# Values and keys of the scans turned by blocks of 32x32 and DMAs instead of on TensorE; the low-rank columns in four groups of output rows

## The chip, the cores and the metric

The kernel runs on one core of a Trainium2 chip. The metric is the device time of one execution in microseconds (us). The kernel before was run three times; the median is what counts. One further execution was taken by the hardware profiler, and all rows of the trace are from that one. Lines written L876 are lines of the kernel before.

## What is computed

The reference is one inference step of a decoder layer: a SwiGLU feed-forward block, a mixer, and a second feed-forward block, each with an RMSNorm before and after. There are 256 prompt tokens and 8 samples of 4 tokens, together 288 columns, and a model width of 2048. The mixer has 4 GLA heads (128 keys, 256 values, decays from 16 low-rank columns) and 8 HGRN heads (128 keys, 128 values). Both are recurrences per head:

```python
# S_t = diag(exp(log_a_t)) S_{t-1} + k_t^T v_t ; o_t = q_t S_t
q, k, v, a_lr, r, hq, hf, hi, hg = jnp.split(proj, _split_points(), axis=-1)
log_alpha = jax.nn.log_sigmoid((a_lr @ gla_w_up + gla_b).astype(jnp.float32)) / GLA_TAU
...
s_new = (jnp.exp(last[:, :, 0, :])[..., None] * s
         + jnp.einsum('bhsd,bhsv->bhdv', ki * jnp.exp(last - cum), vi))
```

The outputs are the tokens and the final states of every head, for the prompt (which starts from zero) and for each sample.

## The kernel before

Activations lie with features on the 128 partitions and the 288 token columns along the free dimension: 16 tiles `x[k]` and 16 tiles `y[k]`. Every large product is done in split fp32: a weight unit of 128x1024 is loaded (`raw`, 512 KB, on SyncE's queue), ScalarE rounds it to `wh` (L96) and VectorE takes the rest `wl` (L97); three matmuls (L548 to L550) then give hi x hi, hi x lo and lo x hi. Three raw units and four split ones are held ahead (`RAW_BUFS`, `HL_BUFS`). `block` (L539) runs four 128-row output tiles over all k tiles of the contraction, and calls `tick(k)` after each k tile. For the last unit of a block the four outputs are finished first, and its ticks follow together.

The mixer's work around the recurrences is done in these ticks. `tick` (L1295) first pops one entry of `turns`, then takes one step of the oldest unfinished generator `scan`, then one entry from each list in `later` that was there at the tick's start. So small matmuls, evacuations and DMAs of a scan are strung between the main matmuls of the next blocks. There are six scans: two of GLA (two heads each) and four of HGRN (two heads each). The order of the projection blocks is qk0, v0, qk1, v1, hfq0, hi0, hfq1, hi1, hfq2, hfq3 and then four gate blocks. A scheduler sets the order of the instructions on each engine from this order of issue and its own estimate of when an operand is ready; each engine then runs its queue in that order, and waits on semaphores.

What the change touches:

- `ev_v` (L892) evacuates a value block of 4 tiles (v0, v1, hi0, hi1). VectorE scales each tile into `y` (L897) and the sample columns, three times over, into `v3` (L898). The entry `turn` then transposes the tile on TensorE with `by_token` (L873): two transposes of 128 prompt tokens (L876) and one of the 96 tripled sample columns (L877). ScalarE copies the result to `Vt` (tokens on partitions) and `V32`, and `stack` (L879) splits the sample part into `Vs`.
- `key_t` and `key_e` (L1139, L1144) do the same for the keys of each of a scan's two heads: three transposes, ScalarE's copy into `kd` (L1148), and `stack` into `ks`.
- `final(a)` (L1181) multiplies `kd` with `Vt` to the prompt's final state, and stores it from GpSimd's queue. It is called in the scan's own steps: for the first head when the second one's keys are turned, for the second head in the scan's last steps. The sample states are stored from GpSimd's queue too (L1206).
- `a_lr` (L1332) forms the low-rank columns in v0's tick 13: 32 matmuls of the split inputs `xh[k]`, `xl[k]` (L1336) with a stationary tile that holds the rounded and the remaining part of the 16 columns. VectorE scales them (L1337), and the split result `alr` feeds `gla_decay` (L1346), whose matmul (L1350) starts the decays.

DMAs are issued by SyncE (weights, states), GpSimd (stores, small loads) and ScalarE (two small loads). The last feed-forward block already turns its input and output by VectorE's transposes of 32x32 blocks (L660, L662) and DMAs that put the blocks in their places (L671, L675).

Of the kernel before, what the change touches and what calls it, by code (L numbers as in the profile page):

```python
# [16 lines left out]
P = 128  # L17
TP = 256
TS = 32
# [106 lines left out]
def trunk_kernel(ctx, tc, x_prompt, x_sample, state_gla, state_hgrn, norm_gains, f1_in, f1_out, f2_in, f2_out,  # L126
# [115 lines left out]
    x = [xpool.tile([P, T], F32, name=f"x{k}") for k in range(KT)]  # L242
    y = [xpool.tile([P, T], F32, name=f"y{k}") for k in range(KT)]
    xh = [xpool.tile([P, T], F32R, name=f"xh{k}") for k in range(KT)]
# [346 lines left out]
    def xrhs(k):  # L591
        return xh[k], xl[k]
# [183 lines left out]
    def mixer(pn, border):  # L776
        with ExitStack() as mx:
# [25 lines left out]

            aw32, alr32 = y[KT - 2:], y[KT - 3]

            ahl = gp.tile([P, 1024], F32R, name="ahl", tag="V")
# [10 lines left out]

            def split_lr():

                av = ahl[:, 0:32 * KT].rearrange("p (k c) -> p k c", c=32)  # L820
                with tc.issue_after(pn.split[0]), tc.issue_after(pn.split[1]):
                    S.activation(av[:, :, 0:16], araw, AF.Copy)
                    V.tensor_tensor(av[:, :, 16:32], araw, av[:, :, 0:16].bitcast(F32), op=ALU.subtract)

# [47 lines left out]

            def by_token(tp, src, src3):  # L873

                for t in range(2):
                    PE.transpose(tp[:, t * P:(t + 1) * P], src[:, t * P:(t + 1) * P], ident)  # L876
                PE.transpose(tp[0:96, TP:TP + P], src3, ident)  # L877

# [6 lines left out]
            def vtiles(nm):  # L885
                vs32.append(vs32.pop(0))
                return (gp.tile([P, 2, 512], F32, name=f"V{nm}", tag="V"), vs32[-1],
                        gp.tile([96, 512], F32R, name=f"Vs{nm}", tag="Vs"))

            turns = []  # L890

            def ev_v(Vt, V32, Vs, y0=8):  # L892
                def ev(f, ps):

                    vt = y[y0 + f]
                    v3 = tmp.tile([P, 3, TS], F32, name="v3", tag="v3", bufs=4)
                    V.tensor_tensor(vt[:, 0:TP], ps[:, 0:TP], rt[:, 0:TP], op=ALU.mult)  # L897
                    V.tensor_tensor(v3, ps[:, TP:T].unsqueeze(1).broadcast_to([P, 3, TS]),  # L898
                                    rt[:, TP:T].unsqueeze(1).broadcast_to([P, 3, TS]), op=ALU.mult)

                    def turn():
                        tp = auxtile("tp_v")
                        by_token(tp, vt, v3.rearrange("p n t -> p (n t)"))
                        c = slice(f * P, (f + 1) * P)
                        S.activation(Vt[:, 0:2, c], tp[:, 0:TP].rearrange("p (t c) -> p t c", c=P), AF.Copy)
                        S.activation(V32[0:TS, c], tp[0:TS, TP:TP + P], AF.Copy)
                        stack(Vs[:, c], tp, TS)

                    turns.append(turn)
                return ev  # L910
# [9 lines left out]
            def scan(d, Vt, V32, Vs, gla, ytile0, s0, sp_out, ss_out):  # L920
# [216 lines left out]
                kds, bds, sqs, pos, mss = {}, {}, {}, {}, {}  # L1137

                def key_t(a):  # L1139
                    tp = auxtile("tp_k")  # L1140
                    by_token(tp, k[:, a, :], K3[:, a].rearrange("p n t -> p (n t)"))
                    return tp

                def key_e(a, tp):  # L1144

                    kd = sp[0].tile([P, 2, P], F32, name="kd", tag="kd")
                    ks = sp[0].tile([96, P], F32R, name="ks", tag="ks")
                    S.activation(kd, tp[:, 0:TP].rearrange("p (t c) -> p t c", c=P), AF.Copy)  # L1148
                    stack(ks, tp, 2 * TS)
                    kds[a] = kd, ks  # L1150

                def apart(a, b0):

                    src = kds[a][1] if gla else Vs[:, a * P:(a + 1) * P]
                    bd = sp[0].tile([96, nb, P], F32R, name="bd", tag="bd")
                    V.tensor_tensor(bd, src.bitcast(F32).unsqueeze(1).broadcast_to([96, nb, P]),
                                    bmask[:, b0:b0 + nb].unsqueeze(2).broadcast_to([96, nb, P]), op=ALU.mult)
                    bds[a, b0] = bd

                def out(a):  # L1160
                    vc = Vt[:, :, a * dv:(a + 1) * dv]

                    po, ss = auxtile("o"), auxtile("os")
                    for j in range(nv):
                        vj = vc[:, :, j * P:(j + 1) * P]
                        c0, c1, c2 = j * TP, j * TP + P, (j + 1) * TP
                        PE.matmul(po[:, c0:c1], vj[:, 0, :], Dg[:, 0, a, :], start=j == 0, stop=True, skip_group_check=True)
                        PE.matmul(po[:, c1:c2], vj[:, 0, :], X[:, a, :], start=False, stop=False, skip_group_check=True)
                        PE.matmul(po[:, c1:c2], vj[:, 1, :], Dg[:, 1, a, :], start=False, stop=True, skip_group_check=True)

                    for b in range(NB):
                        r = slice(b % 4 * TS, (b % 4 + 1) * TS)
                        PE.matmul(ss[r, 0:dv], qm[a][:, b * TS:(b + 1) * TS], states[a, b // nb * nb][:, b % nb, :],
                                  start=b < 4, stop=False, skip_group_check=True)
                    for i in range(4):
                        c = slice(i * dv // 4, (i + 1) * dv // 4)
                        PE.matmul(ss[i * TS:(i + 1) * TS, c], Ds[:, a, :], V32[:, a * dv + c.start:a * dv + c.stop],
                                  start=False, stop=True, skip_group_check=True)
                    pos[a] = po, ss

                def final(a):  # L1181

                    kd, vc = kds[a][0], Vt[:, :, a * dv:(a + 1) * dv]
                    ps = auxtile("st")
                    for t in range(2):
                        PE.matmul(ps[:, 0:dv], kd[:, t, :], vc[:, t, :], start=t == 0, stop=t == 1)
                    st = tmp.tile([P, dv], F32, name="st", tag="st", bufs=1)
                    S.activation(st, ps[:, 0:dv], AF.Copy)
                    G.dma_start(sp_out[a], st)

                def sample(a, b0):

                    s = states.pop((a, b0))
                    ks, bd = kds[a][1], bds.pop((a, b0))
                    ps = auxtile("sn")
# [66 lines left out]
                for a in range(2):  # L1262
                    tp = key_t(a)
                    load_state()
                    if a == 1:
                        final(0)
                        if gla:
                            new_state()
                    yield
# [15 lines left out]
                    new_state()  # L1285
                    if a == 1:
                        final(1)
                    yield
# [43 lines left out]
            def a_lr():  # L1332
                ps = mmtile("a_lr")
                for k in range(KT):
                    for i, m in enumerate(xrhs(k)):
                        PE.matmul(ps[:, 0:T], ahl[:, 32 * k:32 * k + P], m, start=k + i == 0, stop=k + i == KT)  # L1336
                V.tensor_tensor(alr32[0:32, :], ps[0:32, 0:T], rt[0:32, :], op=ALU.mult)  # L1337
                S.activation(alr[0:32, :], alr32[0:32, :], AF.Copy)
# [36 lines left out]
            for g in range(2):  # L1375
# [5 lines left out]
                if g == 0:  # L1381
                    vt = vtiles("g0")
                    block("v0", KT, xrhs, ev_v(*vt), 
                          tick=lambda k: (pn.tick1(k), split_lr() if k == 8 else a_lr() if k == 13 else None))
                    lower_bounds()
                    gla_decay(d, g)
                else:
                    gla_decay(d, g)
                    vt = vtiles("g1")
                    block("v1", KT, xrhs, ev_v(*vt), tick=tick)  # L1390
                gens.append((g, scan(d, *vt, True, 4 * g, state_gla[0][:, 2 * g:2 * g + 2],
                                     sgp[0, 0, 2 * g:2 * g + 2], sgs[0][:, 2 * g:2 * g + 2]), True))
            ds, vts = {}, {}
            for kind, g in HORDER:
                if kind == "hi":
                    written(g)
                    vts[g] = vtiles(f"h{g}")
                    block(f"hi{g}", KT, xrhs, ev_v(*vts[g], 8 + 4 * g), tick=tick)
                else:
                    written(g)  # L1400
                    ds[g] = group_tiles(f"h{g}")
                    block(f"hfq{g}", KT, xrhs, ev_hgrn(ds[g], g), tick=tick)
                for j in list(ds):
                    if j // 2 in vts:
                        c = slice((j % 2) * 256, (j % 2 + 1) * 256)
                        vt, v32, vs = vts[j // 2]
                        gens.append((2 + j, scan(ds.pop(j), vt[:, :, c], v32[:, c], vs[:, c], False, 8 + 2 * j,
                                                 state_hgrn[0][:, 2 * j:2 * j + 2], shp[0, 0, 2 * j:2 * j + 2],
# [113 lines left out]
```

## Time and profile before

| | |
|---|---|
| median of 3 runs | 2257.85 us (2257.52 to 2260.43) |
| the profiled execution | 2256.56 us |
| its span, first to last instruction | 2254.8 us |
| TensorE matmul busy | 2242.7 us, 17868 instructions |
| VectorE busy | 1379.7 us |
| ScalarE busy | 1021.4 us |
| GpSimd busy | 136.1 us |
| granted TensorE clock, mean | 0.998 |

The page's first part gives busy time by engine, its second the span in 40 slices, its fourth the chain of work that ended last. In rows in order of time the columns are: start, duration, engine, line, operation, what it writes and reads, shapes, count, and in brackets the idle time of its engine before it with what ended it. A matmul's duration is from its start to its modelled end; matmuls overlap, so the time that one costs TensorE is the distance to the next one's start. In rows by line the columns are busy us, mean ns of one, and idle time before.

### The profile page before, as it was taken

What the parts mean: (1) busy time and instruction counts of PE and PEld (TensorE: products, weight loads), DVE (VectorE), ACT (ScalarE), POOL (GpSimd) and SP (SyncE); (2) the same over time, 40 slices, a digit from 0 to 9 for tenths busy, and PEclk for the clock granted to TensorE, in tenths of its full rate; (3) what the DMA queues carried; (4) which work ended last, traced back from release to release, by engine and by line L of the source; (5) the groups of instructions that cost most, each with busy time, mean ns of one, the idle gap of its engine ahead of it and who ended that gap; (6) DMA issues with size and microseconds to landing.
All of it is one profiled execution on the core that took longest, in us unless ns stands there. A gap on an engine that the chain in (4) does not pass through costs nothing.

```text
span 2254.8 us, 43365 instructions
## 1 busy us (share of the span) xinstructions
PE 2242.7 (99%) x17868; PEld 2227.0 (99%) x17868; DVE 1379.7 (61%) x2251; ACT 1021.4 (45%) x1575; POOL 136.1 (6%) x250
## 2 busy tenths in 40 slices
PE   9999999999999999999999999999999999999998
PEld 9999999999999999999999999999999999999998
DVE  7545545554565468788888755954555455545646
ACT  6443333333334346555666654544333333333344
POOL 2000000000000001011000000430000000000005
PEclk9999999999999999999999999999999999999999
DMA  7555555555555544556556554665555555555555
GB/s 221 171 163 165 168 167 163 166 168 166 164 167 184 166 165 141 177 175 205 169 170 181 166 183 140 182 188 166 163 167 168 164 164 169 166 164 166 168 164 153
DMA packets 225606, 382.51 MB, mean 170 GB/s; under 512 B 20242, under 2 KB 60224, under 8 KB 225408
## 3 DMA queue, kind: packets, MB, share of 16 engines
q1 hardware_dynamic: 214736, 365.15, 51.0%
q0 software_dynamic: 8496, 14.41, 2.4%
q8 instruction: 140, 2.29, 0.4%
q10 hardware_dynamic: 2176, 0.18, 0.1%
q14 instruction: 58, 0.48, 0.1%
HBM read 363.75 MB, written 11.80 MB: 167 GB/s over the span
## 4 chain that ended last, share of the span: by engine, by line
PE 97%; DVE 2%; ACT 0%; issue 0%; DMA 0%; DVEq 0%; POOL 0%; ACTq 0%; SPq 0%; POOLq 0%
PE gate L548 10%; PE gate L550 9%; PE gate L549 9%; PE up L550 8%; PE up L548 8%; PE up L549 8%; PE out L549 8%; PE out L550 8%; PE out L548 8%; PE mo L550 2%; PE mo L548 2%; PE mo L549 2%; PE hfq L548 1%; PE hfq L550 1%; PE hfq L549 1%; PE qk L548 1%
## 5 line engine op out<-in xcount | busy, mean ns | idle before, releaser
L97 DVE TENSOR_TENSOR wl<-raw,wh 128x1024 fp32r<-128x1024 f32 (+1 forms) x674 | 821.8, 1220 | 620.2 <-ACT wh L96 617.2
L96 ACT ACTIVATE wh<-raw 128x1024 fp32r<-128x1024 f32 (+1 forms) x674 | 711.4, 1056 | 1011.9 <-PE gate L549 311.9
L548 PE MATMUL gate<-xh,wh 128*128 128x288 f32 x1660 | 488.9, 296 | 0.0
L550 PE MATMUL gate<-xh,wl 128*128 128x288 f32 x1660 | 488.7, 295 | 0.0
L549 PE MATMUL gate<-xl,wh 128*128 128x288 f32 x1660 | 485.6, 295 | 0.0
L549 PE MATMUL out<-hl,wh 128*128 128x288 f32 x1408 | 415.6, 295 | 0.0
L550 PE MATMUL up<-xh,wl 128*128 128x288 f32 x1408 | 415.1, 295 | 0.0
L550 PE MATMUL out<-hh,wl 128*128 128x288 f32 x1408 | 415.0, 295 | 0.0
L548 PE MATMUL up<-xh,wh 128*128 128x288 f32 x1408 | 414.8, 295 | 0.1
L549 PE MATMUL up<-xl,wh 128*128 128x288 f32 x1408 | 414.6, 294 | 0.0
L548 PE MATMUL out<-hh,wh 128*128 128x288 f32 x1408 | 413.7, 294 | 0.0
L548 PEld LDWEIGHTS gate<-xh,wh 128*128 128x128 f32 x1660 | 310.9, 188 | 1.2 <-DVE u L626 0.2
L550 PEld LDWEIGHTS gate<-xh,wl 128*128 128x128 f32 x1660 | 311.5, 188 | 0.4 <-DVE wl L97 0.4
L549 PEld LDWEIGHTS gate<-xl,wh 128*128 128x128 f32 x1660 | 310.4, 188 | 0.3
L550 PEld LDWEIGHTS out<-hh,wl 128*128 128x128 f32 x1408 | 264.7, 188 | 0.0
L548 PEld LDWEIGHTS out<-hh,wh 128*128 128x128 f32 x1408 | 264.6, 188 | 0.0
L548 PEld LDWEIGHTS up<-xh,wh 128*128 128x128 f32 x1408 | 264.1, 188 | 0.5 <-ACT g L618 0.3
L549 PEld LDWEIGHTS out<-hl,wh 128*128 128x128 f32 x1408 | 264.4, 188 | 0.0
L550 PEld LDWEIGHTS up<-xh,wl 128*128 128x128 f32 x1408 | 264.2, 188 | 0.0
L549 PEld LDWEIGHTS up<-xl,wh 128*128 128x128 f32 x1408 | 264.1, 188 | 0.1
L706 DVE TENSOR_TENSOR y<-out,y 128x288 f32<-128x288 f32 x288 | 121.2, 452 | 101.3 <-PE out L550 98.3
L548 PE MATMUL hfq<-xh,wh 128*128 128x288 f32 x256 | 77.9, 305 | 0.0
(377 smaller groups left out, 2492.6 us busy)
## 6 DMA issues: line engine op xcount, KB each, us to landing
raw<-in_ffn_w_in_dram SPq DMA_DIRECT2D x351, 512.0 KB, 3.5
raw<-in_ffn_w_out_dram SPq DMA_DIRECT2D x176, 512.0 KB, 3.5
raw<-in_mix_w_in_dram SPq DMA_DIRECT2D x64, 512.0 KB, 3.7
raw<-in_mix_w_in_dram SPq DMA_DIRECT2D x96, 256.0 KB, 3.2
raw<-in_mix_w_out_dram SPq DMA_DIRECT2D x32, 512.0 KB, 3.7
out_dram<-s POOLq DMA_DIRECT2D x32, 256.0 KB, 2.9
s<-in_state_gla_dram SPq DMA_DIRECT2D x16, 256.0 KB, 4.0
s<-in_state_hgrn_dram SPq DMA_DIRECT2D x16, 256.0 KB, 5.0
```

Source lines behind the costliest of these rows:

```text
L96: i1 = self.nc.scalar.activation(h[:, c], raw[:, c], AF.Copy).ins
L97: i2 = self.nc.vector.tensor_tensor(l[:, c], raw[:, c], h[:, c].bitcast(F32), op=ALU.subtract).ins
L548: yield lambda: PE.matmul(dst, w[0][:, c:c + P], parts[0], start=start, stop=False)
L549: yield lambda: PE.matmul(dst, w[0][:, c:c + P], parts[1], start=False, stop=False)
L550: yield lambda: PE.matmul(dst, w[1][:, c:c + P], parts[0], start=False, stop=stop)
L706: V.tensor_tensor(y[k], ps, y[k], op=ALU.add)
```

## The change

The 16 `y` tiles become four tiles of four, with the same names for their parts. Values: `ev_v` evacuates prompt and samples in one operation per tile. For v0, v1 and hi0 VectorE transposes the tile's 32x32 blocks into a spare group of `y`, and 20 DMAs on GpSimd's queue move the blocks to `Vt` and `V32`; then `parts` splits the samples into `Vs` for the whole block. hi1 has no spare group and is still turned on TensorE, with its sample columns once instead of three times. The entries of `turns` are two of transposes, four of moves, four empty ones and `parts`.

```diff
+                def turn32(f):
+                    def run():
+                        for i in (f, f + 1):
+                            V.transpose(b32[:, :, 2 * i:2 * i + 2, :], vg[:, i, 0:TP].rearrange("p (t q c) -> p q t c", t=2, q=4))
+                        if f:
+                            V.transpose(bs32, vg[:, :, TP:T])
+                    return run
+                def move32(b, sample):
+                    rows = cols = slice(b * TS, (b + 1) * TS)
+                    def run():
+                        if sample:
+                            for n in range(4):
+                                r = slice(n * TS, (n + 1) * TS)
+                                G.dma_start(V32[0:TS].rearrange("p (f c) -> p f c", c=P)[:, :, r], bs32[r])
+                        for q in range(4):
+                            G.dma_start(Vt[q * TS:(q + 1) * TS, :, :, cols].rearrange("p f t c -> p (f t) c"), b32[rows, q])
+                    return run
+                def parts():
+                    v = V32[0:TS, :]
+                    S.activation(Vs[0:TS, :], v, AF.Copy)
+                    V.tensor_tensor(Vs[TS:2 * TS, :], v, Vs[0:TS, :].bitcast(F32), op=ALU.subtract)
+                    S.activation(Vs[2 * TS:96, :], v, AF.Copy)
                 def ev(f, ps):
...
+                    V.tensor_tensor(vg[:, f, :], ps, rt, op=ALU.mult)
+                    if spare is None:
+                        turns.append(by_engine(f))
+                    if f == 3:
+                        if spare is not None:
+                            turns.append(turn32(0))
+                            turns.append(turn32(2))
+                            turns.extend(move32(b, b == 0) for b in range(4))
+                            turns.extend([lambda: None] * 4)
+                        turns.append(parts)
```

Keys: the two prompt transposes per head go. VectorE transposes both heads' blocks once per scan, 16 DMAs (half on SyncE's queue, half on GpSimd's) move them into one `kd`, and both `final` calls come at the end of the same list of `later`, ten and eleven ticks after the first keys are turned; by then the ticks mostly belong to the next scan. The sample keys are transposed on TensorE as before.

```diff
+                def key_blocks():
+                    kb = sp[0].tile([P, 4, 4, TS], F32, name="kb", tag="kb", bufs=1)
+                    kd = sp[0].tile([P, 4, P], F32, name="kd", tag="kd", bufs=1)
+                    kds["prompt"] = kd
+                    for a in range(2):
+                        V.transpose(kb[:, :, 2 * a:2 * a + 2, :],
+                                    k[:, a, 0:TP].rearrange("p (t q c) -> p q t c", t=2, q=4))
+                    def move(b):
+                        r = slice(b * TS, (b + 1) * TS)
+                        for n in range(4):
+                            (nc.sync if n % 2 else G).dma_start(kd[n * TS:(n + 1) * TS, :, r], kb[r, n])
+                    later.append([lambda: None] + [lambda b=b: move(b) for b in range(4)] + [lambda: None] * 4 +
+                                 [lambda: final(0), lambda: final(1)])
                 def key_t(a):
                     tp = auxtile("tp_k")
-                    by_token(tp, k[:, a, :], K3[:, a].rearrange("p n t -> p (n t)"))
+                    PE.transpose(tp[0:96, TP:TP + P], K3[:, a].rearrange("p n t -> p (n t)"), ident)
```

Low-rank columns: the 16 columns are scaled by the norm's gain in plain fp32 (`ag`), and the product takes the unsplit `x[k]`. Each k tile writes one of four groups of 16 output rows (at rows 0, 32, 64 and 96), and the four are added afterwards.

```diff
-                    for i, m in enumerate(xrhs(k)):
-                        PE.matmul(ps[:, 0:T], ahl[:, 32 * k:32 * k + P], m, start=k + i == 0, stop=k + i == KT)
-                V.tensor_tensor(alr32[0:32, :], ps[0:32, 0:T], rt[0:32, :], op=ALU.mult)
+                    q = k % 4 * TS
+                    PE.matmul(ps[q:q + 16, 0:T], ag[:, k, :], x[k], start=k < 4, stop=k >= KT - 4)
+                G.memset(alr32[0:32, :], 0.0)
+                S.activation(alr32[0:16, :], ps[0:16, 0:T], AF.Copy)
+                for q in range(TS, P, TS):
+                    V.tensor_tensor(alr32[0:16, :], alr32[0:16, :], ps[q:q + 16, 0:T], op=ALU.add)
+                V.tensor_tensor(alr32[0:16, :], alr32[0:16, :], rt[0:16, :], op=ALU.mult)
```

More of the change, by code (lines that the diff above doesn't have):

```diff
@@ L242, in trunk_kernel @@
     x = [xpool.tile([P, T], F32, name=f"x{k}") for k in range(KT)]
-    y = [xpool.tile([P, T], F32, name=f"y{k}") for k in range(KT)]
+    yg = [xpool.tile([P, 4, T], F32, name=f"y{k}") for k in range(4)]
+    y = [yg[k // 4][:, k % 4, :] for k in range(KT)]
     xh = [xpool.tile([P, T], F32R, name=f"xh{k}") for k in range(KT)]
@@ L871, in group_tiles, with by_token @@
                 return {n: gp.tile([P, 2, T], F32, name=f"{n}_{nm}", tag=n) for n in ("q", "k", "f")}
-            def by_token(tp, src, src3):
+            def by_token(tp, src, src3=None):
                 for t in range(2):
                     PE.transpose(tp[:, t * P:(t + 1) * P], src[:, t * P:(t + 1) * P], ident)
-                PE.transpose(tp[0:96, TP:TP + P], src3, ident)
+                n = TS if src3 is None else 3 * TS
+                PE.transpose(tp[0:n, TP:TP + P], src[:, TP:T] if src3 is None else src3, ident)
             def stack(dst, tp, low):
@@ L886, in vtiles @@
                 vs32.append(vs32.pop(0))
-                return (gp.tile([P, 2, 512], F32, name=f"V{nm}", tag="V"), vs32[-1],
+                return (gp.tile([P, 4, 2, P], F32, name=f"V{nm}", tag="V"), vs32[-1],
                         gp.tile([96, 512], F32R, name=f"Vs{nm}", tag="Vs"))
             turns = []
-            def ev_v(Vt, V32, Vs, y0=8):
-                def ev(f, ps):
[L895 to L909, printed above, removed]
@@ L1181, in final @@
                 def final(a):
-                    kd, vc = kds[a][0], Vt[:, :, a * dv:(a + 1) * dv]
+                    kd, vc = kds["prompt"], Vt[:, a * nv:(a + 1) * nv]
                     ps = auxtile("st")
                     for t in range(2):
-                        PE.matmul(ps[:, 0:dv], kd[:, t, :], vc[:, t, :], start=t == 0, stop=t == 1)
+                        PE.matmul(ps[:, 0:dv].rearrange('p (n c) -> p n c', c=P), kd[:, 2 * a + t, :], vc[:, :, t, :], start=t == 0, stop=t == 1)
                     st = tmp.tile([P, dv], F32, name="st", tag="st", bufs=1)
@@ L1264, in scan @@
                     load_state()
[L1265 to L1268, printed above, removed]
+                    if a == 0:
+                        key_blocks()
+                    elif gla:
+                        new_state()
                     yield
@@ L1285, in scan @@
                     new_state()
-                    if a == 1:
-                        final(1)
                     yield
@@ L1382, in mixer @@
                     vt = vtiles("g0")
-                    block("v0", KT, xrhs, ev_v(*vt),
-                          tick=lambda k: (pn.tick1(k), split_lr() if k == 8 else a_lr() if k == 13 else None))
+                    block("v0", KT, xrhs, ev_v(*vt, 2, 1),
+                          tick=lambda k: (pn.tick1(k), scale_lr() if k == 8 else a_lr() if k == 13 else None))
                     lower_bounds()
@@ L1389, in mixer @@
                     vt = vtiles("g1")
-                    block("v1", KT, xrhs, ev_v(*vt), tick=tick)
+                    block("v1", KT, xrhs, ev_v(*vt, 2, 1), tick=tick)
                 gens.append((g, scan(d, *vt, True, 4 * g, state_gla[0][:, 2 * g:2 * g + 2],
@@ L1397, in mixer @@
                     vts[g] = vtiles(f"h{g}")
-                    block(f"hi{g}", KT, xrhs, ev_v(*vts[g], 8 + 4 * g), tick=tick)
+                    block(f"hi{g}", KT, xrhs, ev_v(*vts[g], 2 + g, None if g else 3), tick=tick)
                 else:
@@ L1406, in mixer @@
                         vt, v32, vs = vts[j // 2]
-                        gens.append((2 + j, scan(ds.pop(j), vt[:, :, c], v32[:, c], vs[:, c], False, 8 + 2 * j,
+                        gens.append((2 + j, scan(ds.pop(j), vt[:, (j % 2) * 2:(j % 2 + 1) * 2], v32[:, c], vs[:, c], False, 8 + 2 * j,
                                                  state_hgrn[0][:, 2 * j:2 * j + 2], shp[0, 0, 2 * j:2 * j + 2],
```

32 lines of the change are left out of this document (21 added, 11 removed).

## The prediction

> **What bounds the kernel now.** I read the page first (its busy shares and the chain that ended last), then the busy time by stretches, then the order of time on TensorE around the instructions that the diff removes, then the queues of VectorE, GpSimd and SyncE in the scans.
>
> ```profile
> span 2254.8 us, 43365 instructions
> PE 2242.7 (99%) x17868; PEld 2227.0 (99%) x17868; DVE 1379.7 (61%) x2251; ACT 1021.4 (45%) x1575; POOL 136.1 (6%) x250
> ...
> PE 97%; DVE 2%; ACT 0%; issue 0%; DMA 0%; DVEq 0%; POOL 0%; ACTq 0%; SPq 0%; POOLq 0%
> ```
>
> TensorE (PE) works 99% of the span and is 97% of the chain. A microsecond less on its queue is a microsecond less of time, unless something else is late in its place. The change lies in the mixer, so what counts is whether PE is as full there. Two stretches from the scans (columns: length, then busy us and count for PE, weight load, VectorE, ScalarE, GpSimd):
>
> ```profile
> 1010.00:1060.00 50.00, 50.00 (x487) 48.04 (x486) 43.04 (x98) 31.42 (x77) 6.81 (x10) 1.00 0.64 192
> 1060.00:1110.00 50.00, 50.00 (x572) 48.13 (x572) 41.24 (x103) 30.89 (x74) 4.12 (x6) 1.00 0.61 182
> ```
>
> PE has no idle time. VectorE (DVE) is next with 41 to 43 of 50 us; GpSimd (POOL) does nearly nothing; the granted clock is 1.00.
>
> **Values turned off PE.** A turn of one value tile before the change, between main matmuls:
>
> ```profile
> 915.48 0.29 PE L550 MATMUL qk<-xh,wl 128*128 128x288 f32 x1
> 915.61 0.38 PE L876 MATMUL tp_v<-ident,y 128*128 128x128 f32 x2
> 915.83 0.27 PE L877 MATMUL tp_v<-ident,v 128*96 128x128 f32 x1
> 915.86 0.38 PE L548 MATMUL qk<-xh,wh 128*128 128x288 f32 x1
> ...
> 916.21 0.29 PE L550 MATMUL qk<-xh,wl 128*128 128x288 f32 x1
> ```
>
> The duration column is latency; what PE pays is the distance of starts. From one L550 to the next is 0.73 us. Three main matmuls fill 0.40 of it (they start 0.13 apart: 915.48, 915.61), so a turn of three transposes costs 0.33. Four tiles in three value blocks (both GLA groups and the first HGRN one) lose it: 12 x 0.33 = **4.0 us**. The fourth block (hi1) keeps its turns, with a third transpose of 32 columns in place of 96; I take that as no change.
>
> **Keys.** The same three transposes per key tile, in 12 tiles (two in each of six scans; the first row groups them, the others are in order of time):
>
> ```profile
> L877 PE MATMUL tp_k<-ident,acc 128*96 128x128 f32 x12 | 3.3, 272 | 0.0
> 952.53 0.30 PE L550 MATMUL v<-xh,wl 128*128 128x288 f32 x1
> 952.66 0.38 PE L876 MATMUL tp_k<-ident,k_g 128*128 128x128 f32 x2
> 952.88 0.27 PE L877 MATMUL tp_k<-ident,acc 128*96 128x128 f32 x1
> ...
> 953.26 0.29 PE L550 MATMUL v<-xh,wl 128*128 128x288 f32 x1
> ```
>
> Again 0.33 us. The two prompt transposes go, the sample one stays: the L876 pair starts at 952.66 and L877 at 952.88, so the pair is 0.22, and 0.11 is left. 12 x 0.22 = **2.6 us**. Bounds: nothing, if a lone transpose costs as much as three, and 4.0 if it costs nothing. I take 2.6, from the starts.
>
> **Low-rank columns.** Now 32 matmuls in split fp32 form, one after another, end to end:
>
> ```profile
> 904.76 0.29 PE L1336 MATMUL a_lr<-xh,ahl 128*128 128x288 f32 x1
> ...
> 908.84 0.29 PE L1336 MATMUL a_lr<-xl,ahl 128*128 128x288 f32 x1
> 908.97 0.29 PE L548 MATMUL v<-xh,wh 128*128 128x288 f32 x1
> ```
>
> 4.21 us. After the change 16 full-fp32 products of 288 columns go to four groups of 16 output rows. The nearest rows are the sample outputs, which are full fp32 and write four 32-row quarters in turn:
>
> ```profile
> 954.59 0.38 PE L1167 MATMUL o<-Dg,Vg 128*128 128x128 f32 x2
> ...
> 955.70 0.39 PE L1169 MATMUL o<-Dg,Vg 128*128 128x128 f32 x2
> 956.02 1.07 PE L1173 MATMUL os<-s,qm 128*32 128x256 f32 x16
> 956.91 0.29 PE L1177 MATMUL os<-vs,Ds 128*32 128x64 f32 x8
> 957.13 0.40 PE L548 MATMUL v<-xh,wh 128*128 128x288 f32 x1
> 957.37 0.29 PE L549 MATMUL v<-xl,wh 128*128 128x288 f32 x1
> ```
>
> L1173 makes eight products and the row counts 16 instructions: a full-fp32 product is two. They take 956.91 - 956.02 = 0.89 us, 0.056 each, at 256 columns. The unquartered L1167 to L1169 start ten instructions of 128 columns in 1.11 us, 0.111 each, so 0.22 at 256: the quarters run four at a time. For a_lr: 32 instructions x 0.056 x 288/256 = 2.0 us. Going in and out of quarters costs about 0.1 ahead (955.70 + 0.22 to 956.02) and 0.2 behind (the last 0.1 of L1177 to 957.13, and 0.24 to L549 in place of 0.13), 0.3 together. 4.2 - 2.3 = **1.9 us** saved. The bounds: 2.2 with no such switch; and with no overlap 32 x 0.111 x 288/128 = 8.0 us, a loss of 3.8. I take 1.9, since the L1173 row is the same kind of work.
>
> The Trainium skill (TensorE: Matmul & The Clock Gate, Part 3: Packing small matmuls) gives 2.38 times for three column tiles of 512 columns, not three; an estimate from that page's rate is 2.5 us in place of 2.0 and a sum half a microsecond smaller. The L1173 row shows nearly no such loss.
>
> Sum on PE: 4.0 + 2.6 + 1.9 = **8.5 us**. The final-state matmuls are as many as before, only later. PE instructions fall by 36 + 24 = 60, to 17808.
>
> **What lies beside PE, and its cover.** DVE gets transposes of 32x32 blocks, and loses other work (the first two rows give min, median and max ns of a line's instructions, the others are from the order of time):
>
> ```profile
> L660 DVE STREAM_TRANSPOSE b<-x x16: 395/403/440, 1427.7 to 1465.9; 128x256 f32<-128x256 f32 x16
> L662 DVE STREAM_TRANSPOSE bs<-x x16: 161/199/205, 1430.0 to 1466.3; 128x32 f32<-128x32 f32 x16
> 911.23 0.41 DVE L897 TENSOR_TENSOR y<-v,rt 128x256 f32<-128x256 f32 x1
> 911.56 0.25 DVE L898 TENSOR_TENSOR v<-v,rt 128x96 f32<-128x96 f32 x1
> 918.86 0.28 DVE L883 TENSOR_TENSOR Vsg<-tp_v,Vsg 32x128 fp32r<-32x128 f32 x1
> 909.17 0.45 DVE L1337 TENSOR_TENSOR y<-a_lr,rt 32x288 f32<-32x288 f32 x1 [1.65 <-PE a_lr L1336]
> 1057.21 0.68 DVE L1156 TENSOR_TENSOR bd<-Vsh,bmask 96x512 fp32r<-96x512 f32 x1
> ```
>
> Keys: 12 x 0.40 = 4.8 us more. A turned value block: 4 x 0.40, one 128-column transpose between 0.20 and 0.40 (0.3), one subtraction of 512 columns (0.68) and four evacuations of 288 columns (0.45), for 4 x (0.41 + 0.25 + 0.28): +0.6, three times. hi1: 4 x 0.45 + 0.68 - 3.76 = -1.3. a_lr: three sums, +1.35. Together +6.7 us over some 380 us of scans, about 0.9 per 50 us: DVE goes from 43 to 44 of 50 at most. ScalarE loses its copies of turned keys and values. So I cost both at nothing; the cover is the four split units that lie ahead of PE. The regrouped y tiles are the same places under other names, and add no instruction.
>
> Moves: per scan eight DMAs on POOL and eight on SyncE (SP), per turned block 20 on POOL; 48 + 60 = 108 on POOL. What such moves do now, by line and by stretches of the final FFN with and without them:
>
> ```profile
> L671 POOL DMA_DIRECT2D xT<-b x64: 582/582/603, 1434.6 to 1484.9; - x64
> DMA to landing us min/median/max: 1.8/3.6/5.5
> 1434.00:1486.00 52.00, 52.00 (x391) 51.66 (x390) 37.45 (x73) 26.75 (x41) 45.85 (x81) 1.00 0.75 210
> 1486.00:1540.00 54.00, 54.00 (x410) 54.00 (x409) 25.46 (x30) 25.19 (x38) 0.02 (x1) 1.00 0.51 170
> ```
>
> The final FFN already makes such moves, 80 of them in 52 us, and DMA rises from 0.51 to 0.75 busy. PE does 391/52 = 7.5 instructions per us with them and 410/54 = 7.6 without. So the crowd on the DMA engines costs PE nothing that shows. 108 x 0.58 = 63 us of POOL is free time.
>
> **Waits that the change adds.** PE waits for kd's landing at a final state, and all main matmuls stand behind it. ScalarE waits for V32 before its two copies in parts, with weight splits behind it. SP's moves wait for DVE's transposes, with weight loads behind them. The first is the dangerous one. A tick is about 12 main matmuls (1.6 us) and the scan's pieces; the last key move is five ticks ahead of the first final state, 8 us, less where a block ends. Needed: two moves on POOL (1.2) and landing (3.6), 4.8 us, and what POOL is behind. Its stores wait for DVE:
>
> ```profile
> 1049.80 0.71 POOL L1206 DMA_DIRECT2D out_dram<-s  x1 [3.64 <-DVE s L1204]
> 1047.70 0.41 DVE L897 TENSOR_TENSOR y<-hi,rt 128x256 f32<-128x256 f32 x1
> 1077.65 0.38 PE L1167 MATMUL o<-Dg,Vh 128*128 128x128 f32 x2
> ```
>
> With 2 us of that it is 7 in 8. For values the tightest block is hi0: evacuated at 1047.7, used at 1077.65, 30 us later. It needs some 4 us to the first move, 20 x 0.58 = 11.6 and 3.6: about 19.
>
> The longer a_lr chain (a copy and three sums of about 0.45 us each, by L1337's row: +1.8 us) delays the decays. Their matmul stood 1.1 us behind its last input (L1339 ends at 911.0, L1350 starts at 912.16):
>
> ```profile
> 910.57 0.45 DVE L1339 TENSOR_TENSOR alr<-y,alr 32x288 fp32r<-32x288 f32 x1
> 912.16 0.43 PE L1350 MATMUL zp<-alr,ahl 96*128 96x288 f32 x2
> ```
>
> Between nothing (it is placed later among main matmuls) and 0.7 us lost once; I take nothing.
>
> **Forecast.** The profiled execution is 2256.56 us with 1.8 around its span; 2256.56 - 8.5 = 2248.1. The median of the runs shown is 1.3 higher, so **2249.4 us**.
>
> **Rivals.**
> 1. Waits of 1 to 2 us in each of six final states, where a block's end shortens the five ticks or DVE keeps POOL: 6 to 12 us back, 2255 to 2261. For it: DVE at 43 of 50. Against: PE's idle column is zero now.
> 2. The quarters don't overlap at 16 rows: a_lr takes 8.0 + 0.3, so 6.0 of the gain goes: 2255. Against it stands L1173.
> 3. Slower: the small moves land late. POOL stands 3.6 behind DVE, the store takes 0.7, two moves 1.2, landing at its longest 5.5: 11 us against 8, so PE stands 3 us in each scan, 18 us in all: 2267 (from 1.4 us a scan it eats the gain, from 2.2 it is slower). Against: the longest of each would have to fall together.
>
> By the Trainium skill (DMA: Bandwidth & Descriptors, Bandwidth) "Transfers under 64 KB are descriptor-dominated", which speaks for the third. These moves are 16 and 32 KB, and the rows of the final FFN agree in latency (3.6 us for 32 KB) but not in a cost to PE.
>
> **Numbers.** A difference of 0.2% (4.5 us, so below 2253.3 or above 2262.4) is about what a measurement of this kernel can tell. Forecast 0.66 (its own range 2247.2 to 2253.3: keys at 4.0, no switch, 0.3 of spread below; one or two small waits above), first rival 0.14, second 0.06, third 0.14. Faster 0.66, same 0.20, slower 0.14. The range reaches over the first two rivals, 2247.2 to 2262.
>
> **What would show it.** Right: a_lr's first start to the next main matmul about 2.2 us; 17808 PE instructions; PE idle still near zero between 910 and 1260; POOL near 199 us busy; everything behind the mixer some 8 us earlier. Wrong: PE idle ahead of st or o put down to DMA, or SP's weight loads late and ScalarE waiting for raw.

## The result, and the profile after

The changed kernel took 2261.63 us (median of 20 runs, 2259.02 to 2265.63), the kernel before 2258.33 us (median of 20). The ratio is 1.0017, 95% interval 1.0011 to 1.0023: about 4 us slower, where 8.5 us faster was forecast. The time lies in the range that was given and on the other side of no change. The two profiles are of executions near the fastest of their kernels (2259.02 us after, 2256.56 before). Of all kernels below, one execution, of the one with the low-rank columns alone, took 12496 us and is left out of its ratio.

The first part and the chain of the page after:

```profile
span 2257.2 us, 43465 instructions
PE 2236.3 (99%) x17808; PEld 2218.7 (98%) x17808; DVE 1383.5 (61%) x2253; ACT 1015.7 (45%) x1531; POOL 196.8 (9%) x359
...
PE 93%; issue 2%; DVE 2%; DMA 1%; ACT 1%; POOL 1%; DVEq 0%; POOLq 0%; ACTq 0%
```

TensorE has 60 instructions less, as the sums had it, and 6.4 us less busy time, and yet the span is 2.4 us longer. The chain says where to look: TensorE was 97% of it and is 93%; issue, DMA, ScalarE and GpSimd have entered. It doesn't say how much: 4% of the span is 90 us, because from a wait the chain is followed back along other engines for as long as those led up to it. Line numbers of the kernel after differ: the main matmuls are now L549 to L551.

The change begins in the block v0 and its effects end before the output projection (mo), so the stretch between their first matmuls is the cleanest measure in a profile; it leaves out the start of the program, which differs by some us from execution to execution (v's first start lies between 875.9 and 879.7 us in the profiles of this document). The rows of v and mo by tile, before and after; the two numbers behind the durations are the first and the last start:

```profile
L548 PE MATMUL v<-xh,wh x128: 288/295/508, 876.0 to 978.9; 128*128 128x288 f32 x128
L548 PE MATMUL mo<-xh,wh x256: 288/295/299, 1294.9 to 1396.3; 128*128 128x288 f32 x128
```

```profile
L549 PE MATMUL v<-xh,wh x128: 288/295/508, 875.9 to 973.9; 128*128 128x288 f32 x128
L549 PE MATMUL mo<-xh,wh x256: 288/295/299, 1297.7 to 1399.2; 128*128 128x288 f32 x128
```

The stretch is 418.9 us before and 421.8 after: +2.9 us, all that the span lost and more.

TensorE's savings are there. Its order of time after, at the low-rank columns and at a key:

```profile
904.53 0.29 PE L551 MATMUL v<-xh,wl 128*128 128x288 f32 x1
904.75 2.13 PE L1386 MATMUL a_lr<-x,y 128*16 128x288 f32 x32
906.81 0.40 PE L549 MATMUL v<-xh,wh 128*128 128x288 f32 x1
907.05 0.29 PE L550 MATMUL v<-xl,wh 128*128 128x288 f32 x1
907.18 0.29 PE L551 MATMUL v<-xh,wl 128*128 128x288 f32 x1
...
949.91 0.30 PE L551 MATMUL v<-xh,wl 128*128 128x288 f32 x1
950.05 0.27 PE L1195 MATMUL tp_k<-ident,acc 128*96 128x128 f32 x1
...
950.42 0.29 PE L551 MATMUL v<-xh,wl 128*128 128x288 f32 x1
```

From L551 to L551 around a_lr are 2.65 us; less 0.40 for three main matmuls, a_lr costs 2.25 instead of 4.21. A key costs 0.51 - 0.40 = 0.11 instead of 0.33. So 2.0 + 2.6 + 4.0 = 8.6 us are off TensorE's queue.

What takes their place is in the waits of TensorE in the mixer (us in total, times, longest). The same view of before has one wait there:

```profile
PE sc L967 <- ACT R L958: 0.3, 1, 0.3
```

And after:

```profile
PE sc L1004 <- DVE R L1080: 2.3, 1, 2.3
PE sc L1004 <- ACT st L1240: 2.3, 1, 2.3
PE hfq L549 <- DVE z L1414: 1.7, 1, 1.7
PE st L1238 <- DMA raw<-in_mix_w_in_dram: 0.8, 2, 0.6
PE zp L1404 <- DVE alr L1393: 0.5, 1, 0.5
PE gate L549 <- DVE z L1470: 0.5, 1, 0.5
PE st L1238 <- PE sc L1034: 0.5, 1, 0.5
PE sc L1004 <- DVE k_h L1067: 0.3, 1, 0.3
PE st L1238 <- issue: 0.2, 1, 0.2
```

That is 9.1 us in ten waits. A wait counts only from the modelled end of the matmul before, 0.29 us after its start, where the next one would have started after 0.13; so each costs some 0.16 more, 1.6 in all. That is 10.7 us, and 10.2 more than before's one wait cost. 8.6 saved less 10.2 waited is a loss of 1.6, and the stretch shows 2.9.

Most of what is missing is in the granted clock. Behind the wait at hfq (1152.43) it falls to 0.50 for 3.4 us, from 1153.3 to 1156.7, where it is 1.00 in the whole stretch of before. Two windows of 2 us; after ScalarE's and GpSimd's busy time come the granted clock, the DMA share and GB/s:

```profile
1154.00:1156.00 2.00, 2.00 (x11) 2.00 (x10) 1.80 (x4) 2.00 (x5) 0.00 (x0) 0.50 0.00 0
1158.00:1160.00 2.00, 2.00 (x17) 2.00 (x16) 0.64 (x5) 1.23 (x2) 0.00 (x0) 1.00 1.02 255
```

The main matmuls start 0.24 us apart in it instead of 0.13. Half the clock for 3.4 us costs an estimated 1.7 us, so the loss comes to 3.3 where 2.9 is measured. The two waits of 2.3 us have no such stretch behind them; why this one has is not shown.

The three longest waits are TensorE behind ScalarE and VectorE. Followed back, each ends at a DMA for which ScalarE stood. ScalarE after, in order of time, around them:

```profile
1046.23 0.38 ACT L1240 ACTIVATE st<-st 128x256 f32<-128x256 f32 x1 [2.78 <-DMA out_dram<-st]
1046.51 1.05 ACT L96 ACTIVATE wh<-raw 128x1024 fp32r<-128x1024 f32 x1
1053.62 0.63 ACT L932 ACTIVATE Vsh<-vs 32x512 fp32r<-32x512 f32 x1 [6.06 <-DMA vs<-y]
1054.15 0.40 ACT L1074 ACTIVATE R<-Q 128x256 f32<-128x256 f32 x1
...
1099.34 0.41 ACT L1079 ACTIVATE R<-Q 128x256 f32<-128x256 f32 x1
...
1103.13 0.28 ACT L1240 ACTIVATE st<-st 128x128 f32<-128x128 f32 x1 [2.57 <-DMA out_dram<-st]
...
1146.36 1.44 ACT L159 ACTIVATE ls<-ls 128x288 f32<-128x288 f32 x4
1150.61 0.28 ACT L1240 ACTIVATE st<-st 128x128 f32<-128x128 f32 x1 [2.81 <-DMA out_dram<-st]
1150.78 0.43 ACT L159 ACTIVATE z<-z 128x288 f32<-128x288 f32 x1
```

Two things can be read here. First, the copy of a second final state (L1240) waits until the store of the first has landed, because `st` has one buffer. Behind it in ScalarE's queue stand the exponentials of the hfq block (1150.78), for which VectorE and then TensorE wait (hfq at 1152.43). At 1103.13 TensorE's score (sc, 1103.46) has had its operand R since 1099.75; the row names the copy of st, and in the code both take their PSUM tile from the same three banks. Second, parts (L932) stands 6.06 us for the samples' moves, and R, which the next score needs, stands behind it.

### The profile page after: what moved, and what is told of

It is laid out like the page before. It is cut to its first block, busy times and chain, and to the rows that moved or that the text cites. A ratio compares the mean times of both kernels' runs of the same rounds, so it can differ in the third digit from the quotient of the medians.

```text
span 2257.2 us, 43465 instructions
## 1 busy us (share of the span) xinstructions
PE 2236.3 (99%) x17808; PEld 2218.7 (98%) x17808; DVE 1383.5 (61%) x2253; ACT 1015.7 (45%) x1531; POOL 196.8 (9%) x359
## 4 chain that ended last, share of the span: by engine, by line
PE 93%; issue 2%; DVE 2%; DMA 1%; ACT 1%; POOL 1%; DVEq 0%; POOLq 0%; ACTq 0%
PE gate L549 10%; PE gate L551 10%; PE gate L550 10%; PE up L551 8%; PE up L549 8%; PE up L550 8%; PE out L550 8%; PE out L551 8%; PE out L549 8%; PE mo L551 2%; PE mo L549 2%; PE mo L550 1%; PE hfq L549 1%; PE hfq L551 1%; PE hfq L550 1%
## 5 line engine op out<-in xcount | busy, mean ns | idle before, releaser
L549 PE MATMUL gate<-xh,wh 128*128 128x288 f32 x1660 | 489.2, 296 | 0.5 <-DVE z L1470 0.5
L551 PE MATMUL gate<-xh,wl 128*128 128x288 f32 x1660 | 488.8, 295 | 0.2 <-DVE wl L97 0.2
L551 PE MATMUL up<-xh,wl 128*128 128x288 f32 x1408 | 415.1, 295 | 0.0
L551 PE MATMUL out<-hh,wl 128*128 128x288 f32 x1408 | 415.0, 295 | 0.0
L549 PE MATMUL up<-xh,wh 128*128 128x288 f32 x1408 | 414.8, 295 | 0.0
L549 PE MATMUL out<-hh,wh 128*128 128x288 f32 x1408 | 413.8, 294 | 0.0
L549 PEld LDWEIGHTS gate<-xh,wh 128*128 128x128 f32 x1660 | 310.9, 188 | 1.8 <-DVE z L1470 0.8
L551 PEld LDWEIGHTS gate<-xh,wl 128*128 128x128 f32 x1660 | 311.5, 188 | 0.6 <-DVE wl L97 0.6
L551 PEld LDWEIGHTS out<-hh,wl 128*128 128x128 f32 x1408 | 264.7, 188 | 0.0
L549 PEld LDWEIGHTS out<-hh,wh 128*128 128x128 f32 x1408 | 264.6, 188 | 0.0
L549 PEld LDWEIGHTS up<-xh,wh 128*128 128x128 f32 x1408 | 264.1, 188 | 0.3
L551 PEld LDWEIGHTS up<-xh,wl 128*128 128x128 f32 x1408 | 264.2, 188 | 0.0
L672 POOL DMA_DIRECT2D zT<-b x40 | 23.2, 586 | 723.3 <-issue 721.6
```

The source lines that it names most:

```text
L549: yield lambda: PE.matmul(dst, w[0][:, c:c + P], parts[0], start=start, stop=False)
L551: yield lambda: PE.matmul(dst, w[1][:, c:c + P], parts[0], start=False, stop=stop)
L672: queues[n % len(queues)].dma_start(dst[q * TS:(q + 1) * TS, 4 * g:4 * g + 4, :, cols].rearrange("p k t c -> p (k t) c"), b32[rows, q])
```

## The experiments

Theory A: ScalarE's queue holds two kinds of copies that wait for DMAs, and the scans' own work stands behind them. Theory B: the final states' matmuls or the weights wait because of the many small DMAs. Theory C: VectorE's added transposes. All kernels are compared with the kernel before on the same chip. The table has each run's ratio with its 95% interval, and the stretch from v to mo in its profile, which is one execution each.

| kernel | ratio to before | interval | v to mo, us | against before |
|---|---|---|---|---|
| before | | | 418.9 | |
| after | 1.0017 | 1.0011 to 1.0023 | 421.8 | +2.9 |
| low-rank columns alone | 0.9996 | 0.9987 to 1.0005 | 418.7 | -0.2 |
| values alone | 0.9994 | 0.9985 to 1.0003 | 419.6 | +0.7 |
| keys alone | 1.0001 | 0.9992 to 1.0010 | 420.0 | +1.1 |
| after, two buffers for st | 0.9982 | 0.9973 to 0.9991 | 415.4 | -3.5 |
| after, parts held | 1.0001 | 0.9992 to 1.0010 | 420.2 | +1.3 |
| after, both mends | 0.9969 | 0.9956 to 0.9981 | 413.2 | -5.7 |
| after, second final state later | 0.9982 | 0.9974 to 0.9991 | 416.8 | -2.1 |
| before, final states together | 1.0000 | 0.9991 to 1.0009 | 419.8 | +0.9 |
| values and low rank, parts held | 0.9981 | 0.9973 to 0.9990 | 414.5 | -4.4 |
| keys alone, two buffers for st | 0.9985 | 0.9976 to 0.9995 | 417.1 | -1.8 |
| both mends, all final states later | 0.9961 | 0.9949 to 0.9974 | 410.9 | -8.0 |

The sum of above (TensorE's saving, its waits with 0.16 us each, less before's one) gives the last column of every row to within 0.7 us, if 1.7 us is added for a stretch at half the clock. Four profiles have one such stretch, each 3.4 us long: after, values alone, parts held, and the second final state later. Each starts within 2 us of the end of a wait of TensorE of 1.7 to 2.8 us; other waits of 1.7 to 2.3 us have none.

**Low-rank columns alone.** The kernel before with the new `scale_lr` and `a_lr` only.

```diff
-                    for i, m in enumerate(xrhs(k)):
-                        PE.matmul(ps[:, 0:T], ahl[:, 32 * k:32 * k + P], m, start=k + i == 0, stop=k + i == KT)
+                    q = k % 4 * TS
+                    PE.matmul(ps[q:q + 16, 0:T], ag[:, k, :], x[k], start=k < 4, stop=k >= KT - 4)
```

> The kernel before with the low-rank columns in four quarters, and nothing else of the change. All theories: TensorE's 4.2 us for a_lr becomes 2.2, less some 0.5 that the decays' matmul waits for its longer chain: 1.5 to 2 us faster than before.

Measured: 0.9996, so between 2.9 us faster and 1.1 slower. The expected 1.5 to 2 us is in the interval and isn't shown by it. In the profile a_lr's saving is there, and a wait of 1.3 us at a score 250 us later takes most of it back; ScalarE had stood 1.8 us for a late weight load ahead of it. One profile can't say if that load is always late.

**Values alone.** The kernel after with keys, final states and low-rank columns as before.

> The kernel before with only the values of three blocks turned by VectorE and DMAs. Theory A (ScalarE's queue stands at copies that wait for DMAs: the copy of a second final state for its single buffer, and parts for V32): 4.0 us less on TensorE, and at most one wait of about 2 us at parts of hi0, so 2 to 4 us faster than before. Theory B (the final states' matmuls or the weights stand because of the many small DMAs): no faster than before, TensorE idle at o or at weights. Theory C (VectorE's added transposes): about 1 us faster, VectorE without idle time in hfq1.

Measured: 0.9994, between 3.4 us faster and 0.7 slower; the stretch is 0.7 us longer, so the 2 to 4 us of theory A are not shown. In its profile the predicted single wait is there, at a score after hi0:

```profile
PE sc L1005 <- ACT R L1080: 2.8, 1, 2.8
```

Its other waits in the mixer are of at most 0.3 us, and none is at o. Behind the wait the granted clock is 0.50 from 1059.0 to 1062.4. So parts delays even without the final states, and the wait and the half clock together take back the 4.0 us.

**Keys alone.** The kernel before with `key_blocks` and the later final states.

> The kernel before with only the keys turned by VectorE and DMAs and both final states in the next scan's steps. Theory A: 2.6 us less on TensorE, and about 2 us lost in each of two or three scans where ScalarE waits for the first final state's store before it can copy the second: 1 to 5 us slower than before, with ScalarE's idle time ahead of st put down to the store. Theory B: as slow, but with TensorE idle ahead of st for the keys' landing. Theory C: 1 to 2 us faster.

Measured: 1.0001, between 1.8 us faster and 2.3 slower; less slow than theory A's middle. ScalarE waits for the store twice, 3.9 us together, and TensorE's rows are 1.3 and 1.2 us behind that and twice 0.5 ahead of st. The first two fit A and the other two B, so A has the larger part; the rows ahead of st don't name the keys' moves, and that it is their landing is not shown.

**Two buffers for st.**

```diff
-                    st = tmp.tile([P, dv], F32, name="st", tag="st", bufs=1)
+                    st = tmp.tile([P, dv], F32, name="st", tag="st", bufs=2)
```

> The kernel after with two buffers for the final state's copy (st) instead of one. Theory A: ScalarE's 9.6 us of waiting for the store goes, and with it TensorE's idle 2.3 and 1.7 us and what follows from a later POOL queue: 4 to 6 us faster than after, at or a little below before. Theories B and C: as after within 1 us.

Measured: 0.9982 where after has 1.0017; the difference is 0.0035, 8 us, and 6.4 us in the stretch. No wait of ScalarE for out_dram<-st is left, and no stretch at half the clock. More than expected, and against B and C: neither the DMAs nor VectorE's work changed.

**Parts held.** The kernel after with parts behind the last weight split that was issued; the single buffer stays.

```diff
+            self.act = i1
             yield i1, i2
...
+                    with tc.issue_after(W.act):
                         S.activation(Vs[0:TS, :], v, AF.Copy)
```

> The kernel after, with the three operations of parts ordered behind ScalarE's last weight split that was issued ahead of them, so that they can't come earlier in ScalarE's queue than that. Theory A: the wait of 6.1 us for V32 in hi0 and TensorE's idle 2.3 us behind it go; the waits at st stay: about 2.5 us faster than after, near before. If only the single buffer of st counts (A without parts): as after within 1 us.

**Both mends.** Two buffers and parts held.

> The kernel after with both: two buffers for st, and parts held behind the last weight split. Theory A: the gains add, 2 us faster than with two buffers alone, so 5 to 7 us faster than before; of the 8.2 us less on TensorE only the decays' wait, kd's landing and the small waits are left out. If a further wait is hidden behind these: as with two buffers alone.

**The second final state later.** One buffer, four empty ticks between the two.

```diff
-                                 [lambda: final(0), lambda: final(1)])
+                                 [lambda: final(0)] + [lambda: None] * 4 + [lambda: final(1)])
```

> The kernel after with one buffer for st, but with the second final state four ticks (some 7 us) later than the first. Theory A: the store has landed by then, so ScalarE doesn't wait for it; 4 to 6 us faster than after, as with two buffers. If it is the room in memory or the order that a second buffer brings, and not the store's landing: as after.

Measured: parts held 1.0001 (3.6 us off by the ratio, 1.6 by the stretch, around theory A's 2.5), both mends 0.9969 (by the stretch the gains add, -5.7; the interval overlaps with that of two buffers alone), the second final state later 0.9982. The last has the same ratio as a second buffer, with one buffer; so what counts is the store's landing between the two copies. With parts held, the 6.1 us of waiting for V32 are gone from ScalarE's list, while its waits for the store are as in after:

```profile
ACT st L1242 <- DMA out_dram<-st: 9.9, 5, 3.2
```

**Final states together.** The kernel before, keys turned on TensorE, only the two final states moved to the places that they have after.

```diff
+                    if a == 0:
+                        later.append([lambda: None] * 9 + [lambda: final(0), lambda: final(1)])
...
-                        final(0)
...
-                    if a == 1:
-                        final(1)
```

> The kernel before with keys still turned on TensorE, but both final states in successive ticks ten and eleven ticks later, as in the kernel after. Nothing is taken off TensorE. Theory A: the same waits for the store of the first, so 3 to 5 us slower than before. Theory B (it is the keys' DMAs): as before within 1 us.

Measured: 1.0000. Theory A's 3 to 5 us slower failed here. ScalarE does wait for the store, but less, 2.8 us in three times instead of 9.6 in four, and TensorE hardly stands behind it. ScalarE at the place where after lost 2.3 us:

```profile
1106.53 0.40 ACT L1042 ACTIVATE R<-Q 128x256 f32<-128x256 f32 x1
1106.84 0.43 ACT L1248 ACTIVATE r<-r 128x288 f32<-128x288 f32 x1
1107.56 1.06 ACT L96 ACTIVATE wh<-raw 128x1024 fp32r<-128x1024 f32 x1 [0.30 <-PE hi L549]
1109.61 0.28 ACT L1190 ACTIVATE st<-st 128x128 f32<-128x128 f32 x1 [0.99 <-DMA out_dram<-st]
```

Here a weight split stands ahead of the copy, and the score (1108.12 in this run) runs before the copy is done. So final states in successive ticks are not enough by themselves: it takes a queue order in which due work stands behind the copy, and the order of after is such a one. A smaller part may be theory B's: the first stores of the third and fourth scan landed 4.6 and 4.4 us after their issue in after, and 4.0 and 3.2 us here. No run separates the two.

**Values and low rank, parts held; keys alone, two buffers.** The two halves of the change, each with its mend.

> The kernel before with the values of three blocks and the low-rank columns as after, keys and final states as before, and parts held behind the last weight split. Theory A: with no final states in successive ticks and no early parts, TensorE's savings come through: 4.0 + 2.0 less 0.5 at the decays, so 5 to 6 us faster than before. If a part of the savings is lost to something else (late weights, VectorE), 2 to 3 us.

> The kernel before with only the keys turned by VectorE and DMAs, and two buffers for st. Theory A: 2.6 us less on TensorE and about 1 us at the keys' landing, so 1 to 2.5 us faster than before and 2 us faster than keys alone with one buffer. Theory C (VectorE's transposes): as before.

Measured: 0.9981 (4.3 us faster) and 0.9985 (3.4 us faster); the stretches are 4.4 and 1.8 us shorter. The first is somewhat short of 5 to 6: a wait of 0.6 at a score, and 3.3 us in which ScalarE stands for weight loads, are left. The second is as theory A has it, by the stretch; against C.

**All final states later.** Both mends, and six empty ticks instead of four between the key moves and the final states.

```diff
-                    later.append([lambda: None] + [lambda b=b: move(b) for b in range(4)] + [lambda: None] * 4 +
+                    later.append([lambda: None] + [lambda b=b: move(b) for b in range(4)] + [lambda: None] * 6 +
```

> The kernel after with two buffers for st, parts held, and the final states two ticks later still. If TensorE's remaining idle 1.0 us ahead of st is the keys' landing, it goes: 0.5 to 1 us faster than with the two mends alone. If it is the place in the order and not the landing, no change.

Measured: 0.9961, 8.8 us faster than before; median 2250.57 us beside 2258.94. Against both mends (0.9969) the intervals overlap, so the step from the one to the other is shown by the profiles only: the waits at st are gone, and the stretch is another 2.3 us shorter, more than the 0.5 to 1 us expected. Its waits of TensorE in the mixer are two:

```profile
PE zp L1406 <- DVE alr L1395: 0.5, 1, 0.5
PE gate L550 <- DVE z L1472: 0.2, 1, 0.2
```

```profile
L550 PE MATMUL v<-xh,wh x128: 288/295/508, 878.1 to 976.1; 128*128 128x288 f32 x128
L550 PE MATMUL mo<-xh,wh x256: 288/295/299, 1289.0 to 1390.4; 128*128 128x288 f32 x128
```

So 8.0 of the 8.6 us saved on TensorE arrive once nothing stands in the way. This version beats both kernels.

## Why the prediction was wrong

- **Values, keys, low-rank columns on TensorE (8.5 us).** Right, term by term: 4.0, 2.6 and 2.0 for 1.9. With the waits removed, the stretch is 8.0 us shorter. The quarters run beside each other at 16 rows too: 32 instructions from 904.75 to 906.81 are 0.064 us each, where 0.063 was worked out; the second rival fell. The Trainium skill's rate (TensorE: Matmul & The Clock Gate, Part 3: Packing small matmuls), by which an estimate was 2.5, fits less well.
- **"So I cost both at nothing" (VectorE and ScalarE).** For VectorE right: busy time rose by 3.8 us where 6.7 had been worked out, and keys with a second buffer are faster in spite of all their transposes. ScalarE has indeed less to do, 1015.7 us instead of 1021.4. But its cost lies in the order of its queue, not in its busy time.
- **"Waits that the change adds": the step that failed.** It named ScalarE's wait for V32 in parts, with weight splits behind it, and gave it no price and no reason for that. Four empty ticks stand ahead of it, and they don't hold it: the scheduler had it in ScalarE's queue straight behind a split at 1046.51, and the first of the samples' moves was issued at 1047.48. They stood behind the stores of the final states in GpSimd's queue:

```profile
1046.90 0.58 POOL L1241 DMA_DIRECT2D out_dram<-st  x1 [2.08 <-ACT st L1240]
1047.48 2.19 POOL L925 DMA_DIRECT2D vs<-y  x4
```

The stores are not what makes the wait long: with two buffers GpSimd hardly stands for them (0.3 us), and ScalarE's wait for V32 is still 6.0 us. Its length is mostly the moves' own 2.2 us of issue and 4.4 to 5.0 us to landing.

- **"The final-state matmuls are as many as before, only later."** True of the matmuls, and it passed over what they bring along. Before, the stores of a scan's two final states are 6 to 10 us apart; after, 3 to 5 (1 to 4 with the second buffer), and with one buffer the copy of the second can't begin until the first has landed. The third scan, before and after:

```profile
1085.25 0.55 POOL L1189 DMA_DIRECT2D out_dram<-st  x1 [0.69 <-ACT st L1188]
...
1093.46 0.55 POOL L1189 DMA_DIRECT2D out_dram<-st  x1 [0.41 <-ACT st L1188]
```

```profile
1098.48 0.55 POOL L1241 DMA_DIRECT2D out_dram<-st  x1 [5.01 <-ACT R L1074]
1103.70 0.55 POOL L1241 DMA_DIRECT2D out_dram<-st  x1 [4.67 <-ACT st L1240]
```

This is the largest single term, 6 to 8 us by the second buffer. That every buffer of a moved step has to be followed to its release was in no step of the prediction.
- **The granted clock**, 1.00 in the rows of the prediction, was taken to stay so. After the waits it was 0.50 once for 3.4 us, some 1.7 us of the loss.
- **The dangerous wait, TensorE at the keys' landing.** If it exists it is small: 0.8 us of idle ahead of st, put down to a DMA (that of a weight load). With the final states two ticks later the stretch gained 2.3 us, more than those rows; part of it may be the other places of ScalarE's copies. The sum of "7 in 8" was too tight at most, and not late by much.
- **The values' margin** was right where it was worked out: TensorE never waited at o. **The longer a_lr chain** cost 0.5 us where 0 to 0.7 was given and nothing taken.
- **The rivals.** The time of the first, 2255 to 2261, came nearly true (2261.63), but by luck, through another mechanism: its waits were of TensorE for a landing, and what stood was ScalarE. The third, also with waits at the final states, fell: the small moves weren't late by 3 us.

What stays open: in after TensorE stands behind two copies that wait for the store (1103.13 and 1150.61), and with the same two final states together in the kernel before it hardly does. The runs show that the order of ScalarE's queue counts, and not why the scheduler came to the one and the other, nor how much of it is stores that land later. When a wait is followed by half the clock is open too.

## What to carry to other kernels

When a step is moved, follow each of its buffers to the DMA or the reader that frees it: two steps that were 6 to 10 us apart could share one buffer, and 3 to 5 us apart they couldn't without a wait. An engine at 45% busy can still set the time, if its queue is in order and an instruction in it waits for a DMA; empty slots in the order of issue don't keep such an instruction back when the scheduler thinks it ready. What helped here was a second buffer, an explicit order behind other work of the same engine, and two ticks more before the reader.

## What the runs showed of the hardware

A store of 64 KB from GpSimd's queue can hold its buffer for far longer than its data would take: from its issue at 1098.48 to the copy that it held up, at 1103.13, are 4.65 us, while 64 KB at the page's mean of 171 GB/s are an estimated 0.4 us. The eight stores of this size landed 1.8 to 4.6 us after issue, 3.1 in the median. The Trainium skill (DMA: Bandwidth & Descriptors, Anatomy of one DMA) puts most of a DMA's fixed cost, about 2.0 us, to the completion receipt, slowest for a target in HBM; the shortest landing agrees with that figure, and the longest is more than twice it. What the longer ones waited for is not shown.

The 32 KB moves of blocks in the scans were landed 4.3 us after issue in the median for the GLA values (3.6 in the final FFN before). TensorE lost nothing to them that shows: while those of the first block ran, between 915 and 935, DMA was 0.78 busy (0.61 before) and TensorE 20.00 of 20 us; and with both mends and later final states it waits for no DMA.

TensorE's granted clock fell to 0.50 for 3.4 us in four of the thirteen profiles, each time shortly behind one wait of 1.7 to 2.8 us (in after 1.74 us at hfq); so such a wait can cost 1.7 us more than its length.
